# One-hot tiles with two interleaved tokens, a lower counted cost for fp16 matmuls, and POOL for the first low parts of U

## The chip, the core and the metric

The kernel runs on one core of a Trainium2 chip. The metric is the device time of one launch in microseconds; the median of several runs is compared. Engines are named as in the profile: PE (TensorE matmuls), PEld (its weight loads), DVE (VectorE), ACT (ScalarE), POOL (GpSimd), SP (SyncE, which here only issues transfers).

## What is computed

One encoder block on 512 tokens of width 1024: latent attention and gated linear attention, a gated merge, and then a product-key retrieval layer (PEER), in which the time of this study lies:

```python
q = (hf @ w_q).reshape(T, PH, 2, PEER_HALF)                      # 8 heads, 2 halves
scores = jnp.einsum('thpd,hpnd->thpn', q, sub_keys)              # 128 keys per half
s, idx = lax.top_k(scores, K)                                    # 16 of 128
cand = s[:, :, 0, :, None] + s[:, :, 1, None, :]
best, pos = lax.top_k(cand.reshape(T, PH, K * K), K)             # 16 of 256
expert = take_along_axis(cand_idx, pos); gate = softmax(best)    # 16 of 16384 experts
a = gelu(einsum('td,thkd->thk', x, u_tab[expert]))
y = einsum('thk,thkd->td', a * gate, v_tab[expert])
```

## The kernel before

Every f32 matmul is made of three f32r matmuls: each operand is split into a high part (ACT, a copy that rounds) and a low part (the difference, DVE or POOL), and hi·hi, hi·lo and lo·hi are summed in PSUM. `split_hi` and `split_lo` do this for weights; `lo_home[0]` says which engine makes the low part.

For 128 of the 512 tokens the retrieval layer gathers the chosen rows of U and V one by one (`gather`, POOL's indirect DMAs and DVE's products and sums). For the other 384 tokens it is dense: the 16384 experts are taken as 128 groups ("experts" below) of 128 rows. For each, PE multiplies the block of U by all 384 tokens (8 steps of contraction, 3 matmuls each, 24 matmuls of 384 columns), ACT applies Gelu, the result is weighted by the gates and multiplied into V (3 blocks of tokens, 2 halves of the width, 3 matmuls of 512 columns each). The gates reach that dense form by the one-hot stage: for eight tokens at a time (an octet, 48 of them) DVE builds fp16 tiles of one-hot rows of the first key index (`e1`) and of the second, times the high and the low part of the gate (`eh`, `el`), and PE multiplies them per token (`spread`): two matmuls of 128 columns for each token, 16 an octet, one weight load each. ACT copies the sums out, and they go to DRAM (`gd`).

The order of the work is written out by hand, with a planner for what fills PE. `Metered` wraps PE and DVE and adds up an estimate of each instruction's time (`_pe_ns`, `_dve_ns`). In routing and in the one-hot stage `fill` issues pieces of U (one step of contraction, 3 matmuls) for as long as PE's account stands behind DVE's. Experts of U that are done there are kept: their activations are written to DRAM (`gad`) and loaded again (`ga`) in the down projection; the others ("fresh") are made within it. `NB[0]` is the number kept, fixed by how far the filling came, and the order of the down projection mixes kept and fresh groups of four evenly. In it, each of 128 steps loads one block of V (512 KB), and gathered rows are spread over the steps.

Just before routing, the loop over the 16 query blocks `wpq` (`proj`, then `product_keys(mt - 1)`: 4 x 5 search instructions on DVE) ends, and `some(P15)`, `product_keys(15)` and `some(3 * NC_D - P15)` run the first three experts of U around the last product keys. A U expert's weights go through three buffers each of raw, high and low.

In the trace, the tiles `x1`, `x2` and the like stand as `x`; the line of nearly all PE and DVE instructions is that of the helper, L162.

Of the kernel before, what the change touches and what calls it, by code (L numbers as in the profile page):

```python
# [13 lines left out]
F16 = mybir.dt.float16  # L14
I32 = mybir.dt.int32
U32 = mybir.dt.uint32
AF = mybir.ActivationFunctionType
# [27 lines left out]
XB = 3  # L45
# [24 lines left out]
C_ID, C_IOTA = 0, 128  # L70
# [70 lines left out]
def _free(x):  # L141

    n = 1
    for d in list(x.shape)[1:]:
        n *= d
    return n
# [33 lines left out]
def _pe_ns(name, args, kw):  # L180
    if name == "transpose":
        return 112.0
    if name != "matmul":
        return 0.0
    out, w = args[0], args[1]
    n = _free(out)
    if w.dtype == F32:
        return 2 * max(112.0, n / 1.2 + 4)
    return max(107.0, n / 2.4) + 13.0


@with_exitstack
def body(ctx, tc, a, out):
    nc = tc.nc
    pe, act, dve, pool, sp = (Metered(nc.tensor, _pe_ns), nc.scalar, Metered(nc.vector, _dve_ns), nc.gpsimd, nc.sync)
    ctx.enter_context(tc.manual_schedule())
    sb = ctx.enter_context(tc.tile_pool(name="sb", bufs=1))
# [8 lines left out]
    def cc(i, n=1):  # L206
        return cst[:, i:i + n]
# [19 lines left out]
    lo_home = [pool]  # L227

    def split_hi():
        i = state["split"]  # L230
        key, _, n, view = queue[i]
        raw = raws.pop(i)
        hi = sb.tile([128, 1024], F32R, name="whi", bufs=WB)
        lo = sb.tile([128, 1024], F32R, name="wlo", bufs=WB)
        act.activation(hi[:, :n], raw[:, :n], AF.Copy)  # L235
        half.append((key, n, view, raw, hi, lo))
        state["split"] += 1
# [18 lines left out]
    def weights(key):  # L256

        while half:
            split_lo()
        while state["split"] < min(pos_of[key] + 2, len(queue)):  # L260
            split_one()
        run(1)
        return ready.pop(key)
# [47 lines left out]
    def pmm(name="pmm"):  # L311
        return ps.tile([128, T], F32, name=name, bufs=4 if name == "pmm" else 2)
# [5 lines left out]
    def tmp(dt=F32, n=T):  # L318
        return tp[0].tile([128, n], dt, name="tmp", bufs=tp[1])
# [80 lines left out]
    def proj(key, xs=None, bank="pmm"):  # L400
        w = weights(key)
        p = pmm(bank)
        acc(p if key[0] != "u" else p[:, GT:], pairs(w, NC_D), xs or hx)
        if key[0] != "u":
            further(key)
        return p
# [72 lines left out]
    for c in range(NC_D):  # L479
        w = weights(("wkv", c))  # L480
# [35 lines left out]
    for tt in range(NT):  # L516
        p = pmm("pst")
# [12 lines left out]
    for i in range(2):  # L530
        p = proj(("w1", 6 + i))
# [14 lines left out]
    for i in range(4):  # L546
        p = proj(("w1", 8 + i))
        t = tmp()
# [68 lines left out]
    for g in range(4):  # L617
        w = weights(("wq", g))
        for i in range(2):
            p = pmm()  # L620
# [9 lines left out]
            else:  # L630
                t = tmp()
# [6 lines left out]
    w = weights("wk")  # L638
    for i in range(4):
        p = pmm()  # L640
# [6 lines left out]
    w = weights("wv")  # L647
    vt = fr.tile([128, NT, 512], F32, name="t7")
    for tt in range(NT):
        ts = slice(tt * 128, (tt + 1) * 128)  # L650
        p = pmm()
# [131 lines left out]
    x2 = fr.tile([128, NC_D, T], F32, name="x16")  # L783
# [10 lines left out]
    for mt in range(8):  # L794
        g = []
        for s in range(2):
            i = 2 * mt + s
            if i in EARLY:
                t = gin.pop(i)
            else:  # L800
                p = proj(("w1", 12 + i))
                t = tmp()
# [5 lines left out]
        w = weights(("wab", mt))  # L808
        for s, y in ((1, yb), (0, ya)):
            p = pmm()  # L810
# [11 lines left out]
    for mt in range(8):  # L822
        p = proj(("wo", mt), mgx)
# [5 lines left out]
        else:  # L829
            q = tmp()  # L830
# [21 lines left out]
    def product_keys(mt):  # L852
        sc = pmm("pk")
        q = qq.pop(mt)
        for tt in range(NT):
            ts = slice(tt * 128, (tt + 1) * 128)
            pe.matmul(sc[:, ts], q[:, ts], keys[:, mt], start=True, stop=True)
        for tt in range(NT):
            x = sc[:, tt * 128:(tt + 1) * 128]
            wk = tmp(n=128)  # L860
            m8, i8 = srt[:, tt, mt], idx[:, tt, mt]
            dve.max(m8[:, 0:8], x)
            dve.max_index(i8[:, 0:8], m8[:, 0:8], x)
            dve.match_replace(wk, m8[:, 0:8], x, NEG)
            dve.max(m8[:, 8:16], wk)
            dve.max_index(i8[:, 8:16], m8[:, 8:16], wk)
# [32 lines left out]
    for mt in range(16):  # L899
        p = proj(("wpq", mt), h2x)  # L900
# [42 lines left out]
    def some(n):  # L943
        for _ in range(n):
            if left[0]:
                e, c = next(todo)
                if c == 2 and state["split"] <= pos_of["u", e] + 2:
                    split_hi()
                if c == NC_D - 1:
                    left[0] -= 1  # L950

    lo_home[0] = dve
    some(P15)
    product_keys(15)
    some(3 * NC_D - P15)
    ax = ExitStack()
    for tt in range(NT):
        dve.tensor_scalar(srt[:, tt], srt[:, tt], r2c[:, tt:tt + 1], None, op0=OP.mult)
# [72 lines left out]
    pr = rx.enter_context(tc.tile_pool(name="pr", bufs=1))  # L1031
# [107 lines left out]

    def onehot(o):  # L1140

        full = [128, 2, 128, 4]
        it = iota[:, None].to_broadcast(full)
        t0 = 8 * o

        def col(x):
            return x[:, t0:t0 + 8].rearrange("p (g t) -> p g t", t=4)[:, :, None, :].to_broadcast(full)

        e1, e2, eh, el = [pr.tile([128, 2, 128, 4], F16, name=n, bufs=XB) for n in ("x1", "x2", "xh", "xl")]
        dve.tensor_tensor(e2, it, col(i2T), op=OP.is_equal)  # L1150
        (pool if o % 4 in PSH else dve).tensor_tensor(el, e2, col(gl), op=OP.mult)
        dve.tensor_tensor(eh, e2, col(gh), op=OP.mult)
        dve.tensor_tensor(e1, it, col(i1T), op=OP.is_equal)
        hot[o] = e1, eh, el

    def spread(o):

        tb, k = divmod(o, SPT)
        if k == 0:
            gst[tb] = pr.tile([128, 128, TB], F32, name="gs", bufs=2)  # L1160
        gs = gst[tb]
        e1, eh, el = hot.pop(o)
        for q in range(2):
            p = ps.tile([128, 4, 128], F32, name="pst" if q else "pk", bufs=2)
            for i in range(4):
                pe.matmul(p[:, i], eh[:, q, :, i], e1[:, q, :, i], start=True, stop=False)
                pe.matmul(p[:, i], el[:, q, :, i], e1[:, q, :, i], start=False, stop=True)
            act.activation(gs[:, :, 8 * k + 4 * q:8 * k + 4 * q + 4], p.rearrange("p t i -> p i t"), AF.Copy,
                           scale=1.0 / GS)
        if k == SPT - 1:  # L1170
            parts = 4 if tb == T // TB - 1 else 1
            n = 128 // parts
            for i in range(parts):
                act.dma_start(gd[:, tb, i * n:(i + 1) * n].rearrange("p i t -> p (i t)"),
                              gs[:, i * n:(i + 1) * n].rearrange("p i t -> p (i t)"))

    up_out()
    split_hi()
    iota = pr.tile([128, 128, 4], F16, name="iota")
    act.activation(iota, cc(C_IOTA, 128)[:, :, None].to_broadcast([128, 128, 4]), AF.Copy)  # L1180
    step = pr.tile([128, TOPK, NS], F16, name="step")
    act.activation(step, cc(C_STEP, TOPK)[:, :, None].to_broadcast([128, TOPK, NS]), AF.Copy)

# [17 lines left out]
    for o in range(O0, NO + 1):  # L1201
        if o < NO:
            if o == O0 or o % 16 == 0:
                for _ in rt or ():
                    fill()
                rt = route(o // 16 + 1) if o // 16 + 1 < NT else None
                rate = 24.0 / (min(16, 16 - o % 16) - 1)
            onehot(o)
            fill()
            due += rate  # L1210
            while due >= 1.0:
                due -= 1.0
                if rt and next(rt, 1):
                    rt = None
                fill()
        if o > O0:
            spread(o - 1)
        gathered(GO)
        fill()
# [18 lines left out]
    while kept or fresh:  # L1238
        x = kept if not fresh or len(kept) * nf >= len(fresh) * nk and kept else fresh
# [202 lines left out]
```

## Time and profile before

| | us |
|---|---|
| three runs: lowest, median, highest | 1697.27, 1702.72, 1703.10 |
| profiled execution | 1697.78 |
| its span | 1695.9 |
| PE, PEld, DVE busy | 1655.2, 1445.6, 1263.6 |
| ACT, POOL busy | 679.0, 575.9 |

A row of the profile names line, engine, operation, output<-input and shape; a matmul's shown duration (some 300 ns for 128 columns) overlaps that of the next, so the distance from start to start tells how long one lasts. "Idle before" names what ended an engine's wait. The DMA share is the time that packets took, as a share of 16 engines' time. The view of busy time by stage gives in each row: the stretch and its us; busy us and instructions of PE, PEld, DVE, ACT and POOL; TensorE's granted clock; the DMA share; GB/s.

### The profile page before, as it was taken

What the parts mean: (1) busy time and instruction counts of PE and PEld (TensorE: products, weight loads), DVE (VectorE), ACT (ScalarE), POOL (GpSimd) and SP (SyncE); (2) the same over time, 40 slices, a digit from 0 to 9 for tenths busy, and PEclk for the clock granted to TensorE, in tenths of its full rate; (3) what the DMA queues carried; (4) which work ended last, traced back from release to release, by engine and by line L of the source; (5) the groups of instructions that cost most, each with busy time, mean ns of one, the idle gap of its engine ahead of it and who ended that gap; (6) DMA issues with size and microseconds to landing.
All of it is one profiled execution on the core that took longest, in us unless ns stands there. A gap on an engine that the chain in (4) does not pass through costs nothing.

```text
span 1695.9 us, 23253 instructions
## 1 busy us (share of the span) xinstructions
PE 1655.2 (98%) x8505; PEld 1445.6 (85%) x8505; DVE 1263.6 (75%) x2535; ACT 679.0 (40%) x999; POOL 575.9 (34%) x362
## 2 busy tenths in 40 slices
PE   7999999999998999999999999999999999999998
PEld 5777657888877999999999988888888888888887
DVE  6725575254889988989894677877788788878885
ACT  5442544244223635454444433333333333333333
POOL 4532233445330111111111243443454443454550
PEclk9999999999998999999999999999999999999999
DMA  5222113434232777787889999999999999999993
GB/s 173 66 74 72 52 67 132 141 130 149 88 100 88 250 242 235 262 274 260 278 299 344 330 313 325 324 338 328 305 371 331 341 365 328 319 364 324 336 332 131
DMA packets 168849, 406.25 MB, mean 240 GB/s; under 512 B 13383, under 2 KB 86216, under 8 KB 167072
## 3 DMA queue, kind: packets, MB, share of 16 engines
q1 hardware_dynamic: 118624, 230.09, 39.8%
q0 software_dynamic: 37008, 134.58, 22.8%
q10 hardware_dynamic: 13104, 40.11, 6.4%
q8 instruction: 66, 1.08, 0.3%
q14 instruction: 47, 0.39, 0.1%
HBM read 357.28 MB, written 47.45 MB: 239 GB/s over the span
## 4 chain that ended last, share of the span: by engine, by line
PE 85%; DVE 9%; issue 2%; ACT 2%; DMA 2%; POOL 0%; SPq 0%; DVEq 0%; POOLq 0%; ACTq 0%
PE pmm L162 54%; PE pk L162 17%; PE pst L162 14%; DVE kd L162 3%; DVE la L162 2%; DVE tmp L162 2%; DVE rB L162 1%; DMA raw<-in_w 1%; DMA gad<-gx 0%; DMA ga<-gad 0%; DVE r L162 0%; POOL wlo L241 0%; DVE act_lo L162 0%; ACT act_hi L322 0%; DVE stat L162 0%
## 5 line engine op out<-in xcount | busy, mean ns | idle before, releaser
L999 POOL DMA_INDIRECT rows<-in_ur,gidx x128 | 170.0, 1328 | 547.0 <-DVE rows L162 445.4
L162 PE MATMUL pmm<-act_hi,whi 128*128 128x384 f32 (+1 forms) x832 | 303.4, 365 | 12.0 <-ACT act_hi L327 8.7
L162 PE MATMUL pmm<-act_hi,wlo 128*128 128x384 f32 (+1 forms) x832 | 294.9, 354 | 8.5 <-DVE wlo L162 8.5
L162 PE MATMUL pmm<-act_lo,whi 128*128 128x384 f32 (+1 forms) x832 | 294.7, 354 | 0.5 <-DVE act_lo L162 0.5
L999 POOL DMA_INDIRECT rows<-in_v,gidx x128 | 205.4, 1605 | 215.3 <-DVE gout L162 172.2
L241 POOL TENSOR_TENSOR wlo<-raw,whi 128x1024 fp32r<-128x1024 f32 (+1 forms) x74 | 175.6, 2376 | 282.8 <-ACT whi L235 246.9
L235 ACT ACTIVATE whi<-raw 128x1024 fp32r<-128x1024 f32 (+1 forms) x202 | 209.6, 1038 | 109.4 <-PE pmm L162 61.9
L162 DVE TENSOR_TENSOR wlo<-raw,whi 128x1024 fp32r<-128x1024 f32 x128 | 156.3, 1222 | 109.5 <-ACT whi L235 109.5
L162 DVE TENSOR_TENSOR vlo<-vraw,vhi 128x1024 fp32r<-128x1024 f32 x128 | 156.3, 1221 | 82.3 <-issue 79.0
L162 PE MATMUL pmm<-vhi,chi 128*128 128x512 f32 x512 | 199.4, 389 | 0.0
L162 PE MATMUL pmm<-vhi,clo 128*128 128x512 f32 x512 | 199.2, 389 | 0.0
L162 PE MATMUL pmm<-vlo,chi 128*128 128x512 f32 x512 | 199.2, 389 | 0.0
L162 PEld LDWEIGHTS pmm<-act_hi,whi 128*128 128x128 f32 x832 | 159.7, 192 | 27.6 <-ACT act_hi L327 8.7
L162 PEld LDWEIGHTS pmm<-act_hi,wlo 128*128 128x128 f32 x832 | 158.7, 191 | 19.2 <-DVE wlo L162 9.5
L162 PEld LDWEIGHTS pmm<-act_lo,whi 128*128 128x128 f32 x832 | 159.1, 191 | 9.3 <-DVE act_lo L162 1.0
L162 DVE SCALAR_TENSOR_TENSOR gout<-rows,gact,gout 128x1024 f32<-128x1024 f32 x128 | 164.1, 1282 | 2.0 <-DMA rows<-in_v,gidx 0.2
L162 DVE SCALAR_TENSOR_TENSOR rows<-rows,hrep 128x1024 f32<-128x1024 f32 x128 | 153.4, 1219 | 0.5 <-DMA rows<-in_ur,gidx 0.5
L162 PE MATMUL pmm<-t,whi 128*128 128x512 f32 x448 | 141.8, 398 | 0.0
L162 PE MATMUL pk<-act_hi,wlo 128*128 128x384 f32 x416 | 139.1, 334 | 0.0
L162 PE MATMUL pk<-act_lo,whi 128*128 128x384 f32 x416 | 139.1, 334 | 0.0
L162 PE MATMUL pk<-act_hi,whi 128*128 128x384 f32 x416 | 139.0, 334 | 0.0
L1258 ACT ACTIVATE vhi<-vraw 128x1024 fp32r<-128x1024 f32 x128 | 133.9, 1048 | 0.8 <-ACT gx L974 0.5
(267 smaller groups left out, 2996.0 us busy)
## 6 DMA issues: line engine op xcount, KB each, us to landing
raw<-in_u SPq DMA_DIRECT2D x128, 512.0 KB, 4.7
vraw<-in_v SPq DMA_DIRECT2D x128, 512.0 KB, 6.7
gt<-gd SPq DMA_DIRECT2D x32, 768.0 KB, 8.5
gd<-gs ACTq DMA_DIRECT2D x11, 2048.0 KB, 7.2
gad<-gx ACTq DMA_DIRECT2D x76, 192.0 KB, 4.6
ga<-gad SPq DMA_DIRECT2D x76, 192.0 KB, 7.0
raw<-in_w SPq DMA_DIRECT2D x28, 512.0 KB, 3.3
raw<-in_wpq SPq DMA_DIRECT2D x16, 512.0 KB, 3.3
```

The lines of the kernel that those rows point to most:

```text
L162: return f(*args, **kw)
L235: act.activation(hi[:, :n], raw[:, :n], AF.Copy)
L241: (lo_eng or lo_home[0]).tensor_tensor(lo[:, :n], raw[:, :n], hi[:, :n], op=OP.subtract)
L999: pool.indirect_dma_start(out=rows[n], out_offset=None, in_=src[v], in_offset=bass.IndirectOffsetOnAxis(ap=gidx[:, j:j + 1], axis=0))
L1258: act.activation(hi, vraw[n], AF.Copy)
```

## The change

Four places change. First, a matmul with fp16 weights is booked on PE's account with `n / 2.4 + 4` ns, 57 for 128 columns, where the general formula gave 120. Second, the switch of `lo_home` from POOL to DVE moves behind the last product keys and the first three experts of U. Third, the one-hot tiles and `iota` take two interleaved tokens for four: an octet is 4 groups of 128 x 2 elements, where it was 2 groups of 128 x 4. The tiles' size is the same. Fourth, `spread` addresses them accordingly: a token's 128 elements lie 4 bytes apart, where they lay 8 apart, in both operands of its matmuls.

```diff
@@ _pe_ns
     if w.dtype == F32:
         return 2 * max(112.0, n / 1.2 + 4)
+    if w.dtype == F16:
+        return n / 2.4 + 4.0
     return max(107.0, n / 2.4) + 13.0
@@ body
-    lo_home[0] = dve
     some(P15)
     product_keys(15)
     some(3 * NC_D - P15)
+    lo_home[0] = dve
@@ onehot
-        full = [128, 2, 128, 4]
+        full = [128, 4, 128, 2]
...
-            return x[:, t0:t0 + 8].rearrange("p (g t) -> p g t", t=4)[:, :, None, :].to_broadcast(full)
+            return x[:, t0:t0 + 8].rearrange("p (g t) -> p g t", t=2)[:, :, None, :].to_broadcast(full)
@@ spread
             for i in range(4):
-                pe.matmul(p[:, i], eh[:, q, :, i], e1[:, q, :, i], start=True, stop=False)
-                pe.matmul(p[:, i], el[:, q, :, i], e1[:, q, :, i], start=False, stop=True)
+                g, t = 2 * q + i // 2, i % 2
+                pe.matmul(p[:, i], eh[:, g, :, t], e1[:, g, :, t], start=True, stop=False)
+                pe.matmul(p[:, i], el[:, g, :, t], e1[:, g, :, t], start=False, stop=True)
@@ body
-    iota = pr.tile([128, 128, 4], F16, name="iota")
+    iota = pr.tile([128, 128, 2], F16, name="iota")
```

On DVE around the last product keys (`la`, `kd` are their values and indices, `wlo` the low part of a U block), the difference is this:

```order
 L162 MAX_INDEX kd_2947<-la_2946,tmp_3994 128x8
-L162 TENSOR_TENSOR wlo_3967<-raw_3815,whi_3966 128x1024
 L162 MAX la_2946<-pk_4031 128x8
 L162 MAX_INDEX kd_2947<-la_2946,pk_4031 128x8
...
 L162 MAX_INDEX kd_2947<-la_2946,tmp_4054 128x8
-L162 TENSOR_TENSOR wlo_4014<-raw_3877,whi_4013 128x1024
-L162 TENSOR_TENSOR wlo_4074<-raw_3939,whi_4073 128x1024
 L162 TENSOR_SCALAR la_2946<-la_2946,r2c_2962 128x256 x4
```

Three low parts leave DVE's queue, one between product keys 14 and 15 and two behind 15. They come to POOL, ahead of its first gathers; before:

```order
44 L241 TENSOR_TENSOR wlo<-raw,whi 128x1024 x26
45 L873 TENSOR_TENSOR t_2953<-cst 128x128 x8
46 L241 TENSOR_TENSOR wlo<-raw,whi 128x1024 x16
47 L999 DMA rows<-in_ur,gidx 128x1024 x64
```

and now:

```order
44 L243 TENSOR_TENSOR wlo<-raw,whi 128x1024 x26
45 L875 TENSOR_TENSOR t_2953<-cst 128x128 x8
46 L243 TENSOR_TENSOR wlo<-raw,whi 128x1024 x19
47 L1001 DMA rows<-in_ur,gidx 128x1024 x64
```

The run of 16 low parts is one of 19; nothing else moves on POOL.

In the one-hot stage, the queue of DVE shows how much U is filled in, since each expert brings one `wlo` (`x2`, `xl`, `xh`, `x1` are the four one-hot tiles of an octet, shown for two of them). Piece of the difference:

```order
-L162 TENSOR_TENSOR x2_5274<-iota_4158,i2T_4142 128x1024
-L162 TENSOR_TENSOR xl_5276<-x2_5274,gl_4144 128x1024
-L162 TENSOR_TENSOR xh_5275<-x2_5274,gh_4143 128x1024
-L162 TENSOR_TENSOR x1_5273<-iota_4158,i1T_4141 128x1024
+L162 TENSOR_TENSOR x2_5287<-iota_4158,i2T_4142 128x1024
+L162 TENSOR_TENSOR xl_5289<-x2_5287,gl_4144 128x1024
+L162 TENSOR_TENSOR xh_5288<-x2_5287,gh_4143 128x1024
+L162 TENSOR_TENSOR x1_5286<-iota_4158,i1T_4141 128x1024
+L162 TENSOR_TENSOR wlo_5301<-raw_5123,whi_5300 128x1024
 L162 MAX_INDEX pos_5148<-best_5147,cand_5082 128x8 x4
-L162 TENSOR_TENSOR wlo_5305<-raw_5123,whi_5304 128x1024
 L162 MATCH_REPLACE cand2_5149<-best_5147,cand_5082 128x50 x4
+L162 TENSOR_TENSOR wlo_5343<-raw_5164,whi_5342 128x1024
```

Behind this octet stands a second low part where there was one. Over the whole stage, the U experts between the first and the last one-hot matmul go from 43.25 to 59.375, and those made before the first matmul with V from 78 to 94.

## Rows read from the trace of the kernel before

**Rows 1.** The page: busy time, share of the span and instructions of each engine.
```profile
PE 1655.2 (98%) x8505; PEld 1445.6 (85%) x8505; DVE 1263.6 (75%) x2535; ACT 679.0 (40%) x999; POOL 575.9 (34%) x362
```

**Rows 2.** Busy time by stage: one-hot stage, trail, down projection.
```profile
632.00:906.00 274.00, 274.00 (x1822) 265.86 (x1822) 244.56 (x534) 133.46 (x200) 41.04 (x36) 1.00 0.80 270
906.00:950.00 44.00, 42.30 (x244) 41.98 (x243) 17.15 (x20) 18.99 (x27) 2.25 (x3) 1.00 0.99 348
950.00:1650.00 700.00, 700.00 (x3373) 615.58 (x3372) 566.96 (x710) 249.83 (x345) 319.88 (x208) 1.00 0.95 334
```

**Rows 3.** Waits of PE from 541 to 1650: total us, times, longest.
```profile
PE pmm L162 <- DVE wlo L162: 1.9, 2, 1.7
```

**Rows 4.** Timeline of PE, first octet: start us, us, engine, operation; first and last matmul.
```profile
631.98 0.29 PE L162 MATMUL pk<-x,xh 128*128 128x128 f16 x1
...
633.74 0.29 PE L162 MATMUL pst<-x,xl 128*128 128x128 f16 x1
```

**Rows 5.** Timeline of PE's weight loads, the same octet.
```profile
631.98 0.11 PEld L162 LDWEIGHTS <-xh 128*128 128x128 f16 x1 [0.16 <-issue]
631.99 0.13 PEld L162 LDWEIGHTS <-xl 128*128 128x128 f16 x1
632.09 0.12 PEld L162 LDWEIGHTS <-xh 128*128 128x128 f16 x1
```

**Rows 6.** Timeline of PE: 16 f32 matmuls with two moving columns.
```profile
109.91 1.95 PE L162 MATMUL pst<-cst,la 128*128 128x2 f32 x16
```

**Rows 7.** Timeline of PE: f32r matmuls of 384 and of 512 columns, first and last.
```profile
1299.76 0.33 PE L162 MATMUL pk<-act_lo,whi 128*128 128x384 f32 x1
...
1301.49 0.34 PE L162 MATMUL pk<-act_hi,wlo 128*128 128x384 f32 x1
104.71 0.39 PE L162 MATMUL pmm<-act_hi,wlo 128*128 128x512 f32 x1
...
107.43 0.40 PE L162 MATMUL pmm<-act_hi,wlo 128*128 128x512 f32 x1
```

**Rows 8.** Groups of DVE's instructions, routing stage: count | busy us, mean ns | idle before.
```profile
L162 DVE TENSOR_TENSOR wlo<-raw,whi 128x1024 fp32r<-128x1024 f32 x24 | 29.2, 1219 | 5.3 <-ACT whi L235 5.3
L162 DVE TENSOR_TENSOR xh<-x,gh 128x1024 f16<-128x1024 f16 x2 | 1.4, 685 | 0.0
L162 DVE TENSOR_TENSOR cand<-la 128x64 f32<-128x64 f32 x6 | 1.3, 218 | 0.0
L162 DVE TENSOR_TENSOR cand<-la 128x128 f32<-128x128 f32 x3 | 0.8, 281 | 0.0
```

**Rows 9.** DMA of the down projection (950 to 1650), then of the trail.
```profile
DMA packets 109111, 233.72 MB, mean 334 GB/s; under 512 B 7578, under 2 KB 61082, under 8 KB 109066
...
DMA packets 9654, 15.32 MB, mean 348 GB/s; under 512 B 608, under 2 KB 7264, under 8 KB 9652
```

**Rows 10.** Timeline around the last product keys, PE and then DVE.
```profile
526.69 0.42 PE L162 MATMUL pmm<-act_hi,whi 128*128 128x384 f32 x1
533.90 0.69 PE L162 MATMUL pmm<-act_hi,wlo 128*128 128x384 f32 x1 [6.62 <-DVE wlo L162]
532.64 1.21 DVE L162 TENSOR_TENSOR wlo<-raw,whi 128x1024 fp32r<-128x1024 f32 x1
540.11 2.34 DVE L162 TENSOR_TENSOR wlo<-raw,whi 128x1024 fp32r<-128x1024 f32 x2
542.37 1.14 DVE L162 TENSOR_SCALAR la<-la,r2c 128x256 f32<-128x256 f32 x4
546.02 1.21 DVE L162 TENSOR_TENSOR wlo<-raw,whi 128x1024 fp32r<-128x1024 f32 x1
```

**Rows 11.** Busy time from 534 to 540 (columns as in rows 2).
```profile
534.00:540.00 6.00, 6.00 (x19) 6.00 (x20) 5.59 (x32) 0.00 (x0) 0.00 (x0) 0.50 0.27 87
```

**Rows 12.** Timeline: POOL's last low part, and the last of three high parts on ACT.
```profile
509.39 2.41 POOL L241 TENSOR_TENSOR wlo<-raw,whi 128x1024 fp32r<-128x1024 f32 x1 [3.99 <-ACT whi L235]
...
525.53 1.06 ACT L235 ACTIVATE whi<-raw 128x1024 fp32r<-128x1024 f32 x1 [3.42 <-issue]
```

More of the change, by code (lines that the diff above doesn't have):

```diff
@@ L1146, in col @@
         def col(x):
-            return x[:, t0:t0 + 8].rearrange("p (g t) -> p g t", t=4)[:, :, None, :].to_broadcast(full)
-        e1, e2, eh, el = [pr.tile([128, 2, 128, 4], F16, name=n, bufs=XB) for n in ("x1", "x2", "xh", "xl")]
+            return x[:, t0:t0 + 8].rearrange("p (g t) -> p g t", t=2)[:, :, None, :].to_broadcast(full)
+        e1, e2, eh, el = [pr.tile([128, 4, 128, 2], F16, name=n, bufs=XB) for n in ("x1", "x2", "xh", "xl")]
         dve.tensor_tensor(e2, it, col(i2T), op=OP.is_equal)
@@ L1178, in body @@
     split_hi()
-    iota = pr.tile([128, 128, 4], F16, name="iota")
-    act.activation(iota, cc(C_IOTA, 128)[:, :, None].to_broadcast([128, 128, 4]), AF.Copy)
+    iota = pr.tile([128, 128, 2], F16, name="iota")
+    act.activation(iota, cc(C_IOTA, 128)[:, :, None].to_broadcast([128, 128, 2]), AF.Copy)
     step = pr.tile([128, TOPK, NS], F16, name="step")
```

## The prediction

> **What bounds the kernel now.** I read the page first, then the busy time by stage, then single rows. TensorE (PE) is busy 98% of the 1695.9 us span and VectorE (DVE) 75% [rows 1], so the question is what each stage does to PE. Behind the product keys come routing, the one-hot stage from 632 to 906, a short trail to 950 and the down projection to 1650; the table by stage shows the last three [rows 2]. PE never idles in the one-hot stage (274.00 of 274) and in the down projection (700.00 of 700); the list of PE's waits after 541 holds 1.9 us in all [rows 3]. Work taken from PE there comes off the end, if nothing else is nearly as full. In the one-hot stage DVE is at 244.56 of 274 and the DMA engines at 0.80; in the down projection the DMA engines are at 0.95 and move 334 GB/s [rows 2]. That is the narrow place once PE has less to do.
>
> The profiled execution took 1697.8 us (span 1695.9 and 1.9 around it), 4.9 below the median of 1702.7. I sum against 1697.8 and add 4.9 at the end.
>
> **Part 1, the one-hot matmuls.** Each octet of tokens has 16 pairs of fp16 weight load and matmul. The first begins at 631.98, the sixteenth at 633.74 [rows 4]: 1.76 us over 15 steps, 117 ns each. 48 octets make 768 pairs, 89.9 us of PE. What sets the 117 ns? The second weight load starts 0.01 us after the first and the third 0.10 after that [rows 5]: a load that finds room is through at once, and the next ones wait for a matmul. So the load is not what lasts; where a 128-column load does last, in the matmuls with two moving columns, 16 of them take 1.95 us, some 113 ns each [rows 6], and there the moving side has nothing to do. For the streaming side the f32r matmuls give the rate with elements 4 bytes apart: 384 columns take 0.173 us (1299.76 to 1301.49 in ten steps), 512 take 0.227 us (104.71 to 107.43 in twelve) [rows 7]. The difference is 0.417 ns a column, so 128 columns stream in 53.4 ns and at half that rate in 106.8. The 117 ns are the half rate and 10 ns beside it. The operands lie 8 bytes apart now and will lie 4 apart, as the f32r ones do. I therefore take 53.4 + 10 = 63 ns a pair. The ends are 66 (the f32r line drawn back to 128 columns: 0.173 us less 256 times 0.417 ns) and 53 with nothing beside it. The saving is 54 x 768 = **41 us** (39 to 49).
>
> [...]
>
> DVE builds four tiles an octet, 685 ns each for 1024 fp16 elements, against 1219 for 1024 f32 [rows 8]. In the new form the column operand repeats one 4-byte word 128 times, where it repeated 8 bytes. The nearest row is the candidate sum, where a 4-byte word is repeated too: 281 ns for 128 elements, 218 for 64, so 0.98 ns an element; from there to the plain f32 tile it is 1.05 (938 ns for 896 more) [rows 8]. Repeating a word costs nothing there. I take 0; the ends are 0 and 1219 - 685 = 534 ns for each of 192.
>
> The iota that ScalarE builds halves; it is one instruction that PE doesn't wait for: 0.
>
> **Part 2, the counted cost.** The planner now books 57 ns for an fp16 matmul instead of 120, 48 us less in all, and fills PE with pieces of U until its account meets DVE's. The order shows it: experts of U between the first and last one-hot matmul go from 43.25 to 59.375, those behind from 61 to 44.875. At 24 matmuls of 0.173 us an expert is 4.16 us, so 16.1 experts, **67 us of PE, move** from the down projection forward. That costs nothing by itself where PE is the bound at both ends. One-hot stage: 179.9 of U, 89.9 of pairs and 4.2 of joints make 274; then 247.0 + 48.4 + 4.2 = 300. DVE has 16.1 low parts of 1.22 us more [rows 8]: 264 of 300, no fuller than before. DMA there gains 16 loads of U (0.524 MB) and 16 stores (0.197 MB): 74 MB become 85.5, 285 GB/s, under what the down projection moves. ScalarE gets 16 more high parts and stores in that stage, SP 16 more loads (494 issues for 478) in the down projection, all beside PE.
>
> The down projection pays. 700 us become 633 of PE work. Its 233.7 MB [rows 9] lose 16 loads of U and gain 16 reloads of kept activations: 228.5 MB. That asks for **361 GB/s**. No stretch of the table reaches that: 334 over this stage, 348 in the trail, where the DMA engines are at 0.99 and 7264 of 9654 packets are under 2 KB [rows 2, 9]; here it is 61082 of 109111, a kinder mix. At 348 the bytes take 657 us, 24 more than PE; at 361 none. I take the middle, **+12**, since the mix is better than the trail's but an even load can't be had. What is late then is a gathered row or a V block, and DVE and ScalarE pass it on to PE.
>
> **Part 3, low parts by POOL.** PE stops at 527.3 for 6.62 us: the low part of the second U expert stands behind product keys 14 on DVE and is made at 532.64 [rows 10]. After that PE has the half clock, 0.50 from 534 to 540 [rows 11], 19 matmuls in 6 us instead of one every 0.173. The low parts of three experts go to POOL, which takes 2.41 us for one and ends its last at 511.8 [rows 12]. The last of their high parts begins at 525.53 and takes 1.06 [rows 12], so the last low is ready by 529.0, before PE asks for it. PE then runs three experts from 526.69 [rows 10] to 539.2. What is late next is the fifth expert's low part, still on DVE. Product keys 15 now follow 14 at 532.64, take 6.3 us (533.85 to 540.11), and behind them lie the 3.65 us from 542.37 to 546.02 [rows 10]: it starts at 542.6 and ends at 543.8. PE waits 4.6 us there and begins that expert at 543.9, where it began it at some 548.8 (540.3 plus two experts and 0.2). That is 4.9 earlier; if the wait halves the clock as the 6.62 did, 2.8 go again. DVE itself is 3.4 earlier. I take **-4** (-1 to -7).
>
> **Sum.** 1697.8 - 41 + 12 - 4 = 1664.8; with 4.9 on top some **1669 us**. Ends of this case: 1702.7 - 49 + 0 - 7 = 1647 and 1702.7 - 39 + 24 - 1 = 1687.
>
> **Rivals.**
> - *The pairs stay at 117 ns.* The stream may take the half rate at any step other than 2 bytes, or the pair may be bound by something that isn't the step. For it: the 113 ns of f32 loads [rows 6] are close to 117, and no row shows fp16 at another step. Against it: the loads' starts [rows 5]. Then 67 us only change place, the one-hot stage goes to 341, and the DMA term stays: 1702.7 - 4 + 12 = 1711 (1700 to 1725). [...]
> - *DVE falls to the f32 rate on one-hot tiles, slower.* 192 tiles at 534 ns more are 103 us; DVE has 264 of 300 and needs 367, so the stage is DVE's: 1669 + 67 = 1736. The place is the column operand of the four products. DVE takes over from 36 us on, 0.19 us a tile, and the time passes that of before from 70 us on, 0.36 us a tile (1669 + 34 = 1703). Against it is the candidate sum [rows 8]. [...]
> - *The down projection is at its DMA limit already* (0.95 [rows 2] and no more). Then only the bytes saved there count, 5.2 MB or 16 us of 67: 1669 + 39 = 1708.
>
> **Chances.** The first case 0.60, pairs unchanged 0.20, DVE slower 0.12, DMA at its limit 0.08. A measurement tells 0.5% from no change, so faster means under 1694.2 and slower over 1711.2. Faster is the first case with the cheap end of DVE's: 0.63. No change takes half of the unchanged pairs and most of the DMA case: 0.16. Slower is the rest: 0.21. The first case's own range is 1647 to 1687; 8 in 10 must reach into the unchanged pairs: 1648 to 1712.
>
> **What would show it.** Right: fp16 matmuls of an octet some 63 ns apart; the four tiles still near 685; the stage some 300 us with PE full; no 6.6 us wait near 527, one of under 5 near 540; the down projection near 645 us with DMA at 0.98 or more and PE waiting in all some 12 us, released by DVE or ScalarE behind a late DMA. Wrong: pairs still at 117, tiles over 0.9 us, or PE full throughout the down projection (then it is 1657) or waiting over 30 us there.

## The result and the profile after

The changed kernel took **1651.92 us** (1650.88 to 1653.26) against 1702.80 (1697.27 to 1703.10) for the kernel before, run beside it: ratio 0.9709, 95% interval 0.9688 to 0.9730. The forecast was 1669, so the change gave 17 us more than the sum. The profiled executions differ by 46.9 us of span (1695.9 and 1649.0). From start to start of PE's matmuls the pieces are:

| from, to | before | after | |
|---|---|---|---|
| start to first one-hot matmul | 631.98 | 626.26 | -5.7 |
| to the last one-hot matmul | 272.4 | 295.6 | +23.2 |
| to the first matmul with V | 47.9 | 49.4 | +1.5 |
| to the last matmul with V | 736.0 | 669.9 | -66.1 |
| to the end | 7.6 | 7.9 | +0.3 |

Not all of the first 5.7 us belong to the change. PE's first matmul of U behind the loop stands ahead of the wait that the change removes, at 526.69 before [rows 10], and now at

```profile
525.22 0.42 PE L162 MATMUL pmm<-act_hi,whi 128*128 128x384 f32 x1
```

From there to the first one-hot matmul it is 105.3 us before and 101.0 after: the change took 4.2 us. The other 1.5 are scatter: in the runs of this document that first matmul of U lies between some 525 and 530, with the low parts on either engine.

The page, against [rows 1]:

```profile
PE 1610.0 (98%) x8505; PEld 1401.5 (85%) x8505; DVE 1257.4 (76%) x2532; ACT 674.0 (41%) x999; POOL 607.9 (37%) x365
```

PE has 45.2 us less to do and is still busy 98% of the span. The busy time by stage, against [rows 2]: one-hot stage, trail, down projection (the last from 970 to 1605, which answers to 950 to 1650).

```profile
626.00:922.00 296.00, 296.00 (x2203) 288.68 (x2202) 263.32 (x550) 149.11 (x231) 40.56 (x36) 1.00 0.84 288
922.00:971.00 49.00, 46.67 (x262) 46.35 (x261) 21.09 (x25) 20.32 (x29) 3.58 (x3) 0.97 0.98 344
970.00:1605.00 635.00, 635.00 (x2996) 550.09 (x2995) 540.33 (x687) 225.92 (x309) 342.94 (x207) 1.00 0.99 356
```

PE is full in both long stages, as it was. In the last one the DMA engines went from 0.95 and 334 GB/s to 0.99 and 356. The bytes, against [rows 9]:

```profile
DMA packets 108318, 226.22 MB, mean 356 GB/s; under 512 B 7487, under 2 KB 62783, under 8 KB 108276
```

PE's waits from 541 to the end of the V matmuls (total, times, longest), against [rows 3], and ACT's wait for V blocks in the down projection:

```profile
PE pmm L162 <- DVE wlo L162: 4.6, 2, 2.3
PE pmm L162 <- DVE vlo L162: 0.2, 1, 0.2
...
ACT vhi L1261 <- DMA vraw<-in_v: 53.1, 21, 7.3
```

The last of these stood so before:

```profile
ACT vhi L1258 <- DMA vraw<-in_v: 0.2, 1, 0.2
```

V blocks do come late now: ACT waits for them 21 times, where it waited once. But of these 53.1 us only 0.2 reach PE. The timeline of PE, first and sixteenth matmul of the first octet, against [rows 4]:

```profile
626.26 0.23 PE L162 MATMUL pk<-x,xh 128*128 128x128 f16 x1
...
627.14 0.22 PE L162 MATMUL pst<-x,xl 128*128 128x128 f16 x1
```

15 steps in 0.88 us are 58.7 ns a pair where they were 117. Over all pairs that follow one another directly the mean went from 117.5 to 58.4: 59.1 x 768 = 45.4 us, PE's whole gain in busy time. The one-hot tiles on DVE, against [rows 8] (duration ns lowest/median/highest, first and last start):

```profile
L162 DVE TENSOR_TENSOR xh<-x,gh x48: 682/685/689, 616.1 to 916.3; 128x1024 f16<-128x1024 f16 x48
```

685 ns, as before. Around the last product keys, against [rows 10, 11 and 12], first PE's two waits, then DVE's end of the keys and its next low part, POOL's last low part, and the busy time from 538 to 546:

```profile
539.49 0.44 PE L162 MATMUL pmm<-act_hi,whi 128*128 128x384 f32 x1 [1.54 <-ACT gx L976]
542.41 0.44 PE L162 MATMUL pmm<-act_hi,wlo 128*128 128x384 f32 x1 [2.31 <-DVE wlo L162]
...
537.50 1.12 DVE L162 TENSOR_SCALAR la<-la,r2c 128x256 f32<-128x256 f32 x4
541.14 1.21 DVE L162 TENSOR_TENSOR wlo<-raw,whi 128x1024 fp32r<-128x1024 f32 x1
...
525.18 2.39 POOL L243 TENSOR_TENSOR wlo<-raw,whi 128x1024 fp32r<-128x1024 f32 x1 [2.09 <-ACT whi L237]
...
538.00:546.00 8.00, 4.20 (x16) 3.90 (x17) 7.49 (x49) 6.70 (x8) 0.00 (x0) 0.84 0.87 284
```

The 6.62 us wait at 527 is gone. Two short ones of 3.85 us together stand near 540, and the clock there is 0.84, where it was 0.50 for six us.

### The profile page after: what moved, and what is told of

It is laid out like the page before. It is cut to its first block, busy times and chain, and to the rows that moved or that the text cites. A ratio compares the mean times of both kernels' runs of the same rounds, so it can differ in the third digit from the quotient of the medians.

```text
span 1649.0 us, 23335 instructions
## 1 busy us (share of the span) xinstructions
PE 1610.0 (98%) x8505; PEld 1401.5 (85%) x8505; DVE 1257.4 (76%) x2532; ACT 674.0 (41%) x999; POOL 607.9 (37%) x365
## 4 chain that ended last, share of the span: by engine, by line
PE 80%; DVE 10%; DMA 5%; issue 2%; ACT 2%; POOL 1%; SPq 0%; DVEq 0%; POOLq 0%; ACTq 0%
PE pmm L162 56%; PE pk L162 12%; PE pst L162 12%; DVE kd L162 3%; DMA vraw<-in_v 2%; DVE la L162 2%; DVE tmp L162 2%; DVE rB L162 1%; DMA rows<-in_v,gidx 1%; DMA raw<-in_w 1%; DMA ga<-gad 0%; DMA gad<-gx 0%; DVE r L162 0%; POOL wlo L243 0%; DVE act_lo L162 0%
## 5 line engine op out<-in xcount | busy, mean ns | idle before, releaser
L162 PE MATMUL pmm<-act_hi,whi 128*128 128x384 f32 (+1 forms) x960 | 345.5, 360 | 13.7 <-ACT act_hi L329 8.9
L162 PE MATMUL pmm<-act_hi,wlo 128*128 128x384 f32 (+1 forms) x960 | 337.4, 351 | 4.6 <-DVE wlo L162 4.6
L162 PE MATMUL pmm<-act_lo,whi 128*128 128x384 f32 (+1 forms) x960 | 336.7, 351 | 0.5 <-DVE act_lo L162 0.5
L1001 POOL DMA_INDIRECT rows<-in_v,gidx x128 | 222.2, 1736 | 158.3 <-DVE gout L162 123.2
L162 PEld LDWEIGHTS pmm<-act_hi,whi 128*128 128x128 f32 x960 | 182.7, 190 | 29.2 <-ACT act_hi L329 8.9
L162 PEld LDWEIGHTS pmm<-act_hi,wlo 128*128 128x128 f32 x960 | 182.5, 190 | 14.8 <-DVE wlo L162 5.3
L162 PEld LDWEIGHTS pmm<-act_lo,whi 128*128 128x128 f32 x960 | 182.8, 190 | 9.3 <-DVE act_lo L162 1.0
L162 DVE SCALAR_TENSOR_TENSOR rows<-rows,hrep 128x1024 f32<-128x1024 f32 x128 | 153.4, 1219 | 0.0
L1287 ACT ACTIVATE chi<-ga 128x384 fp32r<-128x384 f32 x92 | 48.1, 525 | 204.9 <-PE pst L162 132.2
L162 PEld LDWEIGHTS pmm<-vlo,chi 128*128 128x128 f32 x512 | 96.1, 188 | 20.9 <-DVE vlo L162 0.9
L162 PEld LDWEIGHTS pmm<-vhi,clo 128*128 128x128 f32 x512 | 96.1, 188 | 18.6
```

Of the source, the lines that this page charges most:

```text
L162: return f(*args, **kw)
L1001: pool.indirect_dma_start(out=rows[n], out_offset=None, in_=src[v], in_offset=bass.IndirectOffsetOnAxis(ap=gidx[:, j:j + 1], axis=0))
L1287: act.activation(hi, ga[order[n]], AF.Copy)
```

## The experiments

**The three parts one at a time.** Each is compared with the kernel before. The layout alone:

```diff
-        full = [128, 2, 128, 4]
+        full = [128, 4, 128, 2]
...
+                g, t = 2 * q + i // 2, i % 2
+                pe.matmul(p[:, i], eh[:, g, :, t], e1[:, g, :, t], start=True, stop=False)
```

> The one-hot tiles in groups of two, the counted cost and the low parts as before the change. Theory: the distance of the elements sets the time of a pair, so pairs go to 57 to 58 ns; the planner, which still books 120, fills in no more U, PE has some 180 + 45 + 4 = 229 us of work in the one-hot stage and DVE 245, so DVE becomes the bound there: the stage goes from 272 to some 250, PE idles about 20 us in it, and the kernel gains 20 to 25 us (ratio 0.985 to 0.988). Rival, the count only moves work and the layout alone brings the gain: 45 us, ratio 0.973.

Measured: 1675.09 us, ratio 0.9856 (0.9841 to 0.9871). The pairs run at 57 ns, PE is busy 1615.7 us for 1655.2, and the down projection is as long as before (736.0). But the one-hot stage only shrinks from 272.4 to 249.4. Its busy time, and what PE waited for in it:

```profile
630.00:880.00 250.00, 235.42 (x1816) 225.48 (x1815) 242.64 (x533) 127.70 (x199) 40.19 (x35) 0.98 0.84 292
...
PE pk L162 <- DVE x L162: 10.6, 6, 2.7
PE pmm L162 <- DVE wlo L162: 3.6, 3, 1.7
```

DVE is busy 242.64 of 250 us. PE outruns it, stands still for 14.6 us and sees a clock of 0.98. So a cheaper matmul alone turns the stage into DVE's, and some half of the 45 us is lost there.

The counted cost alone, with the pairs still at 117 ns:

```diff
+    if w.dtype == F16:
+        return n / 2.4 + 4.0
     return max(107.0, n / 2.4) + 13.0
```

> Only the counted cost of fp16 matmuls is changed, the tiles stay in groups of four. Theory: 16 experts of U move into the one-hot stage at 117 ns a pair; that stage goes to some 339 us, the down projection loses 66, PE is full in both, so the time is that of before within 4 us. Rival, a DMA-bound down projection costs PE time: 12 to 24 us slower (ratio 1.007 to 1.014).

Measured: 1701.01, ratio 1.0007 (0.9998 to 1.0017). The one-hot stage and the down projection:

```profile
630.00:970.00 340.00, 340.00 (x2203) 331.51 (x2201) 265.05 (x550) 154.78 (x231) 40.49 (x36) 1.00 0.73 252
...
1017.00:1652.00 635.00, 635.00 (x2996) 550.13 (x2995) 541.82 (x690) 224.77 (x308) 337.59 (x208) 1.00 0.99 357
```

67 us of U change place and nothing else happens: the one-hot stage is 339.7 us, the V matmuls span 670.9, PE is full in both. It also shows, without the other two parts, that 357 GB/s at a DMA share of 0.99 costs PE nothing.

The low parts alone:

```diff
-    lo_home[0] = dve
     some(P15)
     product_keys(15)
     some(3 * NC_D - P15)
+    lo_home[0] = dve
```

> Only the three low parts go to POOL. Theory: 5 to 6 us faster (ratio 0.9965 to 0.997), since the first one-hot matmul of the changed kernel came 5.7 us earlier. Rival, the wait behind the product keys is made up for later in routing: within 1 us.

Measured: 1694.58, ratio 0.9964 (0.9951 to 0.9978), 5.8 us by the medians. The interval runs from 4 to 8 us, and the profiled execution is the slowest of the five (1700.27), so the gain is better read from one stretch of it, PE's first matmul of U to the first one-hot matmul:

```profile
529.49 0.42 PE L162 MATMUL pmm<-act_hi,whi 128*128 128x384 f32 x1
...
630.53 0.29 PE L162 MATMUL pk<-x,xh 128*128 128x128 f16 x1
```

101.0 us for the 105.3 of before: 4.2 us, as in the changed kernel.

**The change without the low parts.** The same four lines, put back in the changed kernel.

> The changed kernel with the first three low parts of U given back to DVE, as before: layout and counted cost remain. Theory (the three parts of the change each have their own place; the low parts were worth 5.8 us when moved alone): some 1657 to 1658 us, ratio to the kernel before 0.973 to 0.975, the first one-hot matmul back near 632. Rival (with the new layout and the longer one-hot stage the start of routing no longer counts, since the planner fills what it gained anyway): within 2 us of the changed kernel, ratio 0.970 to 0.972.

Measured: 1657.85, ratio 0.9744 (0.9723 to 0.9766). By the ratios the low parts are worth 0.35% (6 us) behind the other parts too, but this interval and that of the change touch. The trace is clearer:

```profile
529.81 0.42 PE L162 MATMUL pmm<-act_hi,whi 128*128 128x384 f32 x1
...
635.06 0.23 PE L162 MATMUL pk<-x,xh 128*128 128x128 f16 x1
```

The stretch is back at 105.3 us, 4.2 longer than in the change. (The first one-hot matmul comes at 635 and not near 632, since the work ahead of the stretch ended 3 us later in this execution than in that of the kernel before.) The ratios also give the counted cost its price: from 0.9856 (layout) to 0.9744 (layout and count) are 1.12%, **19 us** and clear of the intervals, where the same line alone gave none.

**Which operand's step sets the distance of the pairs.** Two kernels use tiles of two tokens on one side only. `moving_twos` has `e1` in twos, `e2`, `eh` and `el` in fours; `weights_twos` has it the other way round.

```diff
-                pe.matmul(p[:, i], eh[:, q, :, i], e1[:, q, :, i], start=True, stop=False)
+                t = 4 * q + i
+                m = e1[:, t // 2, :, t % 2]
+                pe.matmul(p[:, i], eh[:, t // 4, :, t % 4], m, start=True, stop=False)
```

> The kernel before, with the streamed one-hot tile alone in groups of two (4 bytes apart) and the weight tiles in groups of four (8 bytes). Theory, the stream sets the pair: 57 to 58 ns. Rival, the weight load sets it: 117 ns.

> The reverse: weight tiles in groups of two, the streamed tile in groups of four. Theory, the stream sets the pair: 117 ns. Rival, the weight load sets it: 57 to 58 ns.

Measured, one run each: 1679.32 and 1696.57, beside 1700.85 for the kernel before. Single runs say little of the time; the reading rests on the distances. The timelines of PE, first and sixteenth matmul of the first octet, first of `moving_twos`:

```profile
632.25 0.25 PE L162 MATMUL pk<-x,xh 128*128 128x128 f16 x1
...
633.17 0.22 PE L162 MATMUL pst<-x,xl 128*128 128x128 f16 x1
```

then of `weights_twos`:

```profile
632.11 0.28 PE L162 MATMUL pk<-x,xh 128*128 128x128 f16 x1
...
633.85 0.30 PE L162 MATMUL pst<-x,xl 128*128 128x128 f16 x1
```

61 ns a pair against 116. The moving side decides. With weights 8 bytes apart a pair takes some 3 ns longer (61 for the 58 of the change), and that is all.

**Other steps.** `eights` puts eight tokens side by side (16 bytes between a token's elements, in both operands), `ones` none (2 bytes).

```diff
-        full = [128, 2, 128, 4]
+        full = [128, 1, 128, 8]
```

(and `[128, 8, 128, 1]` for `ones`, with `iota` and the indices of `spread` accordingly).

> The kernel before with one group of eight tokens: elements 16 bytes apart in both operands. If the rate falls with the distance: half of 117's rate, some 220 ns a pair, and the kernel 70 to 80 us slower. Rival, there are two rates only, full up to 4 bytes and half beyond: 117 ns and the time of before. DVE's tiles stay at 685 ns in both.

> The kernel before with each token's tile by itself: elements 2 bytes apart, and a column operand that repeats a single fp16 element. Theory: pairs at 57 to 58 ns, no faster than at 4 bytes, and DVE's tiles at the f32 rate, about 1220 ns, so that DVE sets the one-hot stage and the kernel is 50 to 90 us slower. Rival, DVE keeps 685 ns for a repeated element: 20 to 25 us faster, like the two-token layout alone.

Measured, one run each: 1828.51 and 1777.61, 128 and 77 us slower than the 1700.85 of the kernel before. The second was expected; the first is far more than the 70 to 80 us of its theory, and the last section takes it up. First and sixteenth matmul, and the one-hot tiles on DVE, of `eights`:

```profile
634.92 0.43 PE L162 MATMUL pk<-x,xh 128*128 128x128 f16 x1
...
638.46 0.41 PE L162 MATMUL pst<-x,xl 128*128 128x128 f16 x1
...
L162 DVE TENSOR_TENSOR xh<-x,gh x48: 683/685/689, 624.8 to 1016.2; 128x1024 f16<-128x1024 f16 x48
```

and of `ones`, with its one-hot stage:

```profile
630.04 0.23 PE L162 MATMUL pk<-x,xh 128*128 128x128 f16 x1
...
630.89 0.22 PE L162 MATMUL pst<-x,xl 128*128 128x128 f16 x1
...
L162 DVE TENSOR_TENSOR xh<-x,gh x48: 1217/1219/1221, 621.0 to 976.4; 128x1024 f16<-128x1024 f16 x48
...
630.00:980.00 350.00, 262.28 (x1810) 246.43 (x1809) 344.04 (x544) 128.17 (x199) 58.29 (x35) 0.90 0.61 210
```

| step of the moving elements | 2 bytes | 4 | 8 | 16 |
|---|---|---|---|---|
| pair, median ns | 56 | 57 | 118 | 234 |
| DVE tile, ns | 1219 | 685 | 685 | 685 |

From 4 bytes up the time of a pair is proportional to the step in these runs, as far as 16; at 2 next to nothing more is gained. DVE is the mirror image: a tile whose repeated unit is one fp16 element costs 1219 ns, 534 more, the time of as many f32 elements [rows 8]. `ones` is the slower rival of the prediction made real, one step further on than the change went: DVE is busy 344.04 of 350 us and PE waits.

**Low parts for longer on POOL.** In the changed kernel `lo_home` goes to DVE only after five low parts, within routing.

```diff
     some(3 * NC_D - P15)
-    lo_home[0] = dve
...
             fill()
+            if left[0] < 125:
+                lo_home[0] = dve
```

> The changed kernel, with the low parts of the fourth and fifth expert made by POOL too. Theory: the two waits of 2.3 and 1.5 us that PE has left around 540, and the half clock behind them, go: 3 to 6 us under the changed kernel, ratio 0.967 to 0.969 to the kernel before. Rival, routing is bound by DVE's chain and PE only waits later: as the changed kernel, 0.971.

Measured: 1654.60, ratio 0.9728 (0.9715 to 0.9741), no gain over the change (0.9709). PE's waits with their releasers, from its timeline between 536 and 575:

```profile
543.94 0.44 PE L162 MATMUL pmm<-act_hi,whi 128*128 128x384 f32 x1 [1.51 <-ACT gx L975]
549.73 0.44 PE L162 MATMUL pmm<-act_hi,wlo 128*128 128x384 f32 x1 [0.98 <-POOL wlo L243]
555.19 0.45 PE L162 MATMUL pmm<-act_hi,wlo 128*128 128x384 f32 x1 [0.64 <-DVE wlo L162]
560.33 0.44 PE L162 MATMUL pmm<-act_hi,wlo 128*128 128x384 f32 x1 [0.64 <-DVE wlo L162]
565.75 0.45 PE L162 MATMUL pmm<-act_hi,wlo 128*128 128x384 f32 x1 [0.97 <-DVE wlo L162]
```

The 2.31 us wait becomes four of 3.2 us in all: PE has no lead left there, and every expert waits for its own low part, whichever engine makes it. The planner, whose account of DVE is shorter by those parts, also fills in 0.875 of an expert less before the first octet. So the first one-hot matmul comes 98.1 us behind the first matmul of U, 3.0 earlier than in the change, but that piece of an expert, 3.6 us of PE, has only been put off. The theory fell.

**How far the DMA engines go.** In the changed kernel PE's filling may run 40 us of its account further ahead of DVE's.

```diff
-LEAD = 3000.0
+LEAD = -37000.0
```

> The changed kernel with PE's filling let run ahead of DVE in routing by 40 us of its account: 14 more experts of U are made before the first one-hot matmul, the one-hot stage keeps its 59.25, and 31.0 experts instead of 44.875 stay behind it. From the first to the last matmul with V that takes some 58 us of PE off the 669.7 us of the changed kernel, and 4.6 MB off the bytes, so that the down projection asks for some 384 GB/s where it now moves 356 at a DMA share of 0.99. Theory (a share of 0.99 still had room, up to the 377 GB/s that the best 100 us of the changed kernel moved, and no further): the stage lasts some 588 us where PE has 612 less waits, so 0 to +15 us over the changed kernel, PE waiting up to 15 us in it; ratio to the kernel before 0.970 to 0.980. Rival A (0.99 and 356 GB/s is the end of what DMA moves here): 222 MB take 623 us, some 45 us over: about 1697, ratio 0.995 to 1.0. Rival B (DMA is nowhere near an end): PE stays full and the time is that of the changed kernel within 3 us, ratio 0.969 to 0.973. Against all of them, waits of PE in routing, where it now runs ahead, would come on top and show as a stretch there.

Measured: 1671.25, ratio 0.9825 (0.9809 to 0.9842), 19 us slower than the change. By the traces the first one-hot matmul comes 58.3 us later, but trail and V matmuls together are only 35.8 shorter. Busy time from 1040 to 1600, PE's waits there, and ACT's for V blocks:

```profile
1040.00:1600.00 560.00, 551.98 (x2501) 463.89 (x2501) 493.07 (x641) 195.42 (x267) 323.81 (x197) 0.99 1.02 371
...
PE pmm L162 <- ACT vhi L1261: 3.2, 2, 1.9
PE pmm L162 <- DVE vlo L162: 3.1, 6, 0.6
PE pmm L162 <- DVE clo L162: 1.8, 2, 1.2
...
ACT vhi L1261 <- DMA vraw<-in_v: 186.6, 67, 8.0
```

Now ACT waits 186.6 us for V blocks (53.1 in the change), the lateness reaches PE, and its clock drops to 0.99. Three stretches of this stage show when:

```profile
1140.00:1240.00 100.00, 100.00 (x465) 85.62 (x465) 90.08 (x115) 35.94 (x48) 59.62 (x36) 1.00 1.04 388
1240.00:1340.00 100.00, 100.00 (x465) 85.66 (x464) 89.47 (x122) 37.14 (x51) 58.45 (x37) 1.00 1.04 383
1440.00:1540.00 100.00, 96.14 (x416) 78.02 (x415) 93.26 (x119) 33.75 (x48) 62.52 (x38) 0.98 1.02 378
```

At 388 and 383 GB/s PE is still full for 200 us; it waits only later, at much the same rate. So the late blocks cost nothing at once, and 371, a mean over all this, is no sharp limit. Rival A, with 356 as the end, falls, and so does rival B. The theory had the place right and the size short, 19 us for at most 15. The spans differ by 22 us. From start to start, all of it lies in the matmuls with V: they last 21 us longer than at 0.227 us each [rows 7], in the change 0.3 longer. Idle time before them is 10.5 of the 21; the rest is matmuls that lasted longer, 20 of them 0.42 us or a little more, and was not taken apart further.

## Why the prediction was right, and by how much it was off

- **The forecast case held.** Pairs got cheaper, DVE tiles did not change, PE stayed the bound in both long stages, and 0.9709 is clearly faster.
- **Part 1, the pairs: right mechanism, 5 ns off.** 53.4 + 10 = 63 ns was forecast, 58.4 came, a saving of 45 us for 41. The runs with one operand changed confirm that the stream, not the load, lasted 117 ns: 61 with the moving side alone at 4 bytes, 116 with the weights alone. What failed is the fixed addition of 10 ns. Steps of 16, 8 and 4 bytes give 234, 118 and 57: the overhead halves with the step, so halving the 117 would have given 58.5.
- **The rival with unchanged pairs** is out: 8 bytes took 118 ns a pair for 57 at 4 and 56 at 2, so a step over 2 bytes does not by itself bring the half rate.
- **DVE at no cost: right.** 685 ns before and after, though the column operand now repeats a 4-byte word. Single repeated fp16 elements in `ones` did cost 534 ns a tile.
- **Part 2, the moved U: right.** The stage became 295.6 us for 300, and the 3.5 us of cheaper pairs account for most of that; DVE 263.32 of 296 was forecast as 264 of 300. That moving costs nothing by itself is the 1.0007 of the counted cost alone. What the prediction left unsaid is that without it part 1 is worth only 24.5 us (1.44%), since DVE then sets the stage.
- **The DMA term of +12: this step failed.** 361 GB/s was asked for, by 228.5 MB in 633 us; 226.22 MB at 356 moved in 635 us with PE full. The bound of 348 was taken from the trail, at a share of 0.99. But neither figure was the end: with the extra filling 388 and 383 GB/s left PE full for 200 us. And lateness is not yet a wait: ACT's 53 us left PE 0.2. What took them up, buffers or ACT's own idle time (it is busy 225.92 of 635 us), was not tested. The term was worth 0, the low end of its range. PE full throughout the down projection, "then it is 1657", stood among the prediction's signs of being wrong.
- **Part 3, the low parts: right.** -4 was forecast, and from PE's first matmul of U to the first one-hot matmul 4.2 us went, in both surroundings; the medians' 6 agree within their intervals. The next late thing was named rightly, the fifth expert's low part. DVE came to it 15.9 us behind that first matmul of U (541.14 less 525.22), as forecast (542.6 less 526.69), and PE went on at 17.2 (542.41), as forecast (543.9). Only the wait came in two pieces: 2.31 us for the low part, and 1.54 ahead of it for ACT's `gx`, which the prediction did not have.

Together, between profiled executions 1664.8 was summed and 1650.9 came. Of these 14 us, 12 are the DMA term, 4 the pairs and 1.5 the earlier start of that first matmul of U; some 4 go the other way, since the stages from the first one-hot matmul on lasted that much longer than pairs and moved U alone make them. The rest of the 17 us is scatter: the sum adds the 4.9 by which the profiled execution before lay under its median, and the one after lay 1.0 under its own.

## What to carry to other kernels

Lay out the moving operand of a matmul so that its elements lie at most 4 bytes apart (for 128 columns of fp16 57 ns a pair, and 118 at 8); the weights' step hardly matters, 3 ns between 4 and 8 bytes. Interleave on DVE's side just as far as its tiles need to keep their time, here two fp16 elements (685 ns a tile, as with four and eight; 1219 with one). When a matmul in a balanced stage gets cheaper, tell the planner too: the layout alone kept half of its gain, and the line that gave nothing by itself was worth 19 us with it. Before booking a cost for a DMA limit, look whether the lateness would reach the bound engine at all: here 53 us of ACT's waits cost PE 0.2. And read a gain of a few us from the stretch that the edit touches, not from the whole time: work ahead of it moved by 5 us from one execution to the next.

## What the runs showed of the hardware

In `eights` the clock fell though PE never waited. In the one-hot stage PE is busy without a gap (395.00 us of 395), yet its mean clock over it is 0.89, where the kernel before shows 1.00 [rows 2]. The sixteen slow pairs of one octet begin at 705.21, and the last at 708.74; the busy time in two stretches, one with the first twelve, the next with the last four and what follows:

```profile
704.00:708.00 4.00, 4.00 (x20) 2.86 (x20) 3.93 (x8) 0.60 (x1) 0.00 (x0) 1.00 0.39 131
708.00:712.00 4.00, 4.00 (x16) 3.71 (x15) 3.67 (x7) 1.09 (x2) 1.15 (x1) 0.57 0.44 180
```

and two matmuls of U there, from PE's timeline:

```profile
709.26 0.52 PE L162 MATMUL pmm<-act_lo,whi 128*128 128x384 f32 x1
709.58 0.52 PE L162 MATMUL pmm<-act_hi,wlo 128*128 128x384 f32 x1
```

The first twelve pairs run at 234 ns with a granted clock of 1.00; the f32r matmuls that follow stand 0.32 us apart, where they took 0.173 at full clock [rows 7], and the stretch shows 0.57. So the strided stream cost twice in this run: 768 pairs are 90 us longer than at 8 bytes, yet the stage grew by 123. The rest lies in the U matmuls of the stage, on average 216 ns apart where they were 178. This is one run, and the expectation, which had counted only the pairs, missed it.
